# Gated products that stay in PSUM, and 512-token products with the second weights, in a two-layer diffusion block

## The chip, the cores and the metric

The kernel runs on one core of one Trainium2 chip, in one launch. The metric is the device time of that core in microseconds (us); lower is better. Three timed runs of the kernel before the change gave 1726.34, 1726.85 and 1729.16 us, a median of 1726.85. The profile is of one further execution, which took 1731.67 us.

The engines are TensorE (PE in the profile; its weight loads are PEld), VectorE (DVE), ScalarE (ACT), GpSimd (POOL) and SyncE (SP, which issues the transfers). A matmul writes PSUM, 2 KB per partition and bank, eight banks. Everything else lives in SBUF. In this kernel GpSimd is given SBUF operands only.

## The reference, cut to what matters

Two layers over 512 latent tokens and 256 context tokens, 1024 features. Each layer mixes tokens (Fourier, retention and neighbourhood attention) and then runs a gated feed-forward with 2816 inner features:

```python
def swiglu(h, w1, w3, w2):
    return (jax.nn.silu(h @ w1) * (h @ w3)) @ w2

x = x + ga_f * swiglu(rmsnorm(x, g_ffn[i]) * (1.0 + sc_f) + sh_f, w1[i], w3[i], w2[i])
```

The first layer does this for latent and context tokens (768), the last for the 512 latent tokens alone. All inputs and outputs are fp32.

## The kernel before, in words

**Precision.** Every fp32 operand is split into a high part, a cast to the matmul's fp32r type, and a low part, the operand less the high part. `mm3` (L398 to L400) then runs three matmuls: high by high, low by high, high by low. Splitting a weight tile is one ScalarE cast (L183) and one subtraction (L188), on GpSimd for most tiles and on VectorE for a few that a table names.

**The two first weights.** The feed-forward's 22 chunks of 128 inner features go in parts of two or four chunks (`FFN_PARTS`: the second part of the first layer and the fifth of the last have two, all others four). For each part, the weight is taken in two by two blocks (halves of the 1024 features by two chunks) and the tokens in two halves, and each of `w1` and `w3` is multiplied by the seven-product scheme of Strassen and Winograd. A job is one weight's pair of chunks; its products come in the order 1, 2, 6, 7, 4, 5, 3 (`STEPS`). Each product is four `mm3`, twelve matmuls, over n tokens: n is 384 in the first layer and 256 in the last. The weight sums that the scheme needs are formed on VectorE (L225 to L229) before they are split.

**After a product.** `complete` (L1586 on) takes each product out of its PSUM bank. Product 1 is copied to SBUF by ScalarE (L1592). Products 6 and 7 are added to the running sums U (L1596, L1599). Products 2, 4, 5 and 3 each finish one block of the result and call `block`; product 5 is also added to U after that (L1604). For `w1`, `block` adds U (L1630) and takes the SiLU on ScalarE (L1631); this is the gate. For `w3` it adds U into a new SBUF tile `gu` (L1634), multiplies that by the gate into a second `gu` (L1635), and `put` splits the outcome into the two halves of `g`: cast on ScalarE (L1461), subtraction (L1462) on VectorE for products 2 and 3 and on GpSimd for products 4 and 5.

**The second weights.** `plain` multiplies a finished part of `g` by `w2` for one eighth m of the output features: for each stream of tokens in `self.out`, one PSUM bank, `mm3` over the part's chunks, and `add_x` (L1658), which adds the scaled result to x. The streams are 512 and 256 tokens in the first layer and 256 and 256 in the last. Eighths 0 and 1 are taken together, stream by stream; 2 to 7 one at a time. The last part of each layer goes through `finish` and `residual` instead (tile `res`).

**Order.** Each engine runs its instructions in the order in which the program emits them. A planner (`in_order`) fixes the order of products; it lets the first products of the next part's jobs go ahead of the `w2` products of a finished part. `WeightStream` emits, as room in a ring of tiles allows, the transfer of each weight, its cast and its subtraction; so on ScalarE the casts of weights and the casts of `g` stand in one queue, and on VectorE the sums for weights, the adds out of PSUM and the subtractions of `g`. In the first layer VectorE also computes the last layer's modulation (L522) between them.

Of the kernel before, what the change touches and what calls it, by code (L numbers as in the profile page):

```python
# [101 lines left out]
class WeightStream:  # L102
# [19 lines left out]
    def add(self, key, ap, callback=None):  # L122
        self.tasks.append((key, callback, len(self.units)))
        self.units.append(ap)
# [219 lines left out]
def run(*gens):  # L344
    for g in gens:
        for _ in g:
            pass


class Kern:  # L350
# [500 lines left out]
    def strips_ahead(self, layer, heads):  # L851

        if heads[0] == 0:
            self.strip_dram = self.dram.tile([4, P, S_END], F32, tag="strips", bufs=2, name=self.nm("strips"))
            self.strip_parts = ((0, S_CC), (S_CX, S_END))
        parts = [x for x in STRIPS if x[0] != "cc"]
        deltas = []
        for name, lo, hi in parts:
            deltas.append(self.act(cols=hi - lo, name="delta"))
            self.nc.sync.dma_start(deltas[-1], self.a["delta"][:, lo:hi])  # L860
        yield
        for h in heads:
            for (name, lo, hi), delta in zip(parts, deltas):
                st = self.act(cols=hi - lo, name="strip")
                run(self.strip_piece(layer, h, name, delta, st))
                yield
                self.nc.sync.dma_start(self.strip_dram[h, :, lo:hi], st)
# [448 lines left out]
    def residual(self, keys, src, x, layer, part, streams, after, norm, order, n, waiting, hook=None, paces=(1, 2, 2, 2), raws=3):  # L1316
# [11 lines left out]
        def one(w, m, st, last, steps=0):  # L1328
            ps = self.ps("res")
            run(self.products(ps, w, src, st, order, order))  # L1330
            if steps:
                norm.step(steps)
            put(ps, m, st)
            if last:
                self.w.done(keys[m])
# [3 lines left out]
        for ps, w, m, st in waiting:  # L1339
            if hook:  # L1340
                hook()
            run(self.products(ps, w, src, st, order[n:], order))
            put(ps, m, st)
            if st is streams[-1]:
                self.w.done(keys[m])
# [18 lines left out]
class FeedForward:  # L1364
# [134 lines left out]
    def prepare(self):  # L1499
# [10 lines left out]
        for i in range(5):  # L1510
            if i < 4:
                ts = [(j, self.scaled(rs, st, j)) for j in (i, i + 4)]
            if i > 0:
                b11, b12, b21, b22 = (block(e, i - 1) for e in range(4))
                v.tensor_sub(b11, b12, b11)
                t2 = self.k.tmp(name="T2")[:, :n]
                v.tensor_sub(t2, b22, b11)
            if i < 4:
                for j, t in ts:
                    self.shifted(t, st, j)  # L1520
            if i > 0:
                hi, lo = self.operand(6, i - 1)
                nc.scalar.copy(hi, t2)
                nc.gpsimd.tensor_sub(lo, t2, hi.bitcast(F32))  # L1524
                nc.gpsimd.tensor_sub(b21, b21, t2)
            yield 0
        for i in range(4):
            v.tensor_sub(block(1, i), block(3, i), block(1, i))
        del b11, b12, b21, b22, t2, t, ts
        for p, e in ((7, 1), (4, 2), (5, 0), (3, 3)):  # L1530
            for i in range(4):
                self.put(self.operand(p, i), block(e, i), i % 2)
                if p == 5:
                    self.h[i] = None
                elif p == 3:
                    self.h[i + 4] = None
            yield 0
# [46 lines left out]
    def complete(self, job, p, ps):  # L1584

        if p == 6 and job.key in self.waiting:  # L1586
            self.complete(job, 2, self.waiting.pop(job.key))
        add = self.k.nc.vector.tensor_add
        ps, u = ps[:, : self.n], job.u
        if p == 1:  # L1590
            u[2] = self.place(job, 0)
            self.k.nc.scalar.copy(u[2], ps)  # L1592
        elif p == 2:
            self.block(job, 0, 0, ps, u[2])
        elif p == 6:
            add(u[2], u[2], ps)  # L1596
        elif p == 7:
            u[3] = self.place(job, 1)
            add(u[3], u[2], ps)  # L1599
        elif p == 4:  # L1600
            self.block(job, 1, 0, ps, u[3])
        elif p == 5:
            self.block(job, 1, 1, ps, u.pop(3))
            add(u[2], u[2], ps)  # L1604
        else:
            self.block(job, 0, 1, ps, u.pop(2))

# [14 lines left out]
    def block(self, job, r, c, ps, u):  # L1622

        k, n = self.k, self.n
        nc = k.nc
        x, q, i = job.key
        sl = slice(n * c, n * c + n)
        gate = self.gate(job, r)[:, sl]
        if x == "w1":
            nc.vector.tensor_add(gate, ps, u)  # L1630
            nc.scalar.activation(gate, gate, AF.Silu)  # L1631
            return
        t, g = (k.tmp(name="gu")[:, :n] for _ in range(2))
        nc.vector.tensor_add(t, ps, u)  # L1634
        nc.vector.tensor_mul(g, t, gate)  # L1635
        if c == 1:
            del self.gates[q, i, r]
        self.put([self.chunk(q, self.parts[q][1] * r + i, p)[:, sl] for p in range(2)], g, r == 1)

    def chunk(self, q, pos, half):  # L1640

# [20 lines left out]
    def plain(self, q, ms):  # L1662

        k = self.k
        ws = [k.w.get(("w2", self.layer, q, m)) for m in ms]
        size = self.parts[q][1]
        order = sorted(range(2 * size), key=lambda i: i % size)
        for st in self.out:
            sl = slice(st[0], st[0] + st[1])
            for m, w in zip(ms, ws):  # L1670
                ps = k.ps("f2")
                for i in order:
                    c = slice(P * i, P * i + P)
                    k.mm3(
                        ps[:, : st[1]],
                        (w[0][:, c], w[1][:, c]),
                        [self.chunk(q, i, p)[:, sl] for p in range(2)],
                        i == order[0],
                        i == order[-1],
                    )  # L1680
                self.add_x(ps, m, st)
        del ws, w
        for m in ms:
            k.w.done(("w2", self.layer, q, m))

    def run(self, acc, hook=None):


        k = self.k
        self.cur, self.waiting, self.gates = None, {}, {}  # L1690
        k.w.max_raws, k.w.max_parts = 5, 6
        k.w.lead, k.w.dve = DVE[self.layer]
        todo = self.order[:-NK]
        self.first_products()
        for i, (job, p) in enumerate(todo[2 * self.lead :]):
            if i % 2:
                next(self.prep, None)
            if i == SPARE_AT:
                k.w.spare = SPARE if self.last else 0
            if i == 5:  # L1700
                acc.clear()
                if self.layer == 0:
                    k.silu_tables()
            if job.key[0] == "m":

                if p != 1:
                    self.plain(job.key[1], (p,) if p else (0, 1))
            else:
                self.product(job, p)
                if job is todo[-1][0]:  # L1710
                    del self.t[p]
                    if hook and p == 6:
                        hook()
# [449 lines left out]
def _layout(x, c, ctx, c_ctx, w_ada, b_ada, g_mix, w_in, ret_decay_logit, ret_norm_g, w_four,  # L2163
# [45 lines left out]
    wf = w_four.reshape(n, 2, P, 256).transpose(0, 2, 1, 3).reshape(n, P, 512)  # L2209
    o["w_four"] = np.concatenate([wf, np.broadcast_to(dft64, (n, P, 256))], axis=-1)  # L2210
    rows = np.concatenate([np.arange(256), 256 + plain, np.arange(640, 1024)])
    o["w_out"] = A(w_out[:, rows].reshape(n, 8, P, P, NK).transpose(0, 4, 2, 1, 3).reshape(n, NK, P, 1024))
    o["w1"], o["w3"] = chunks(w1), chunks(w3)
# [33 lines left out]
```

## Time and profile before

| What | Value |
|---|---|
| Timed runs, median (lowest to highest) | 1726.85 us (1726.34 to 1729.16) |
| Profiled execution | 1731.67 us |
| Its span | 1729.9 us |
| TensorE matmuls busy | 1620.8 us (94%) |
| VectorE busy | 1219.4 us (70%) |
| GpSimd busy | 876.6 us (51%) |
| ScalarE busy | 743.9 us (43%) |
| Mean granted TensorE clock | 0.976 |

Busy time of TensorE counts a matmul from its start to its modelled end, and successive matmuls overlap, so the number that tells its pace is the distance between starts. The feed-forward of the first layer runs from about 470 to 1010 us of the span, that of the last from about 1340 to the end.

### The profile page before, as it was taken

To read this page: it belongs to the slowest core of one execution; us is meant where nothing else is said; L and a number is where in the kernel's file an instruction comes from. 1 tells how busy PE (TensorE), PEld (TensorE's weight loads), DVE (VectorE), ACT (ScalarE), POOL (GpSimd) and SP (SyncE) were. 2 spreads that over 40 slices of the span, in tenths; PEclk is the share of its full clock that TensorE was granted. 3 is DMA by queue.
4 is the path that set the end of the run, shared out by engine and by line. 5 is a ranking of instruction groups with operands and counts; after the bars stand their busy time and mean duration, and the time that the engine had idled before them with its cause. 6 is when DMAs were issued, how large, how long until landed. Compare 5 with 4: busy or idle time off the path is not lost. (4 is left out here: it accounts for less than half of the span.)

```text
span 1729.9 us, 27017 instructions
## 1 busy us (share of the span) xinstructions
PE 1620.8 (94%) x10054; PEld 1474.1 (85%) x10054; DVE 1219.4 (70%) x2040; ACT 743.9 (43%) x1437; POOL 876.6 (51%) x645
## 2 busy tenths in 40 slices
PE   6989999999979997999999999999998799999997
PEld 4867788879878987898989997788788699999997
DVE  6866566762887899586877867665767876767585
ACT  5544445653643323242333553444545544334343
POOL 3333232123575657465666832543145777667673
PEclk9999999999989999999999999999999899999998
DMA  9354253452123343344343444422141232232222
GB/s 347 137 196 135 69 154 96 117 196 99 37 69 115 95 159 106 116 131 126 134 134 116 148 164 132 143 72 89 62 147 52 71 123 86 74 110 86 79 85 70
DMA packets 76387, 202.33 MB, mean 117 GB/s; under 512 B 12704, under 2 KB 19488, under 8 KB 75872
## 3 DMA queue, kind: packets, MB, share of 16 engines
q1 hardware_dynamic: 76256, 200.60, 35.7%
q8 instruction: 80, 1.31, 0.3%
q14 instruction: 51, 0.42, 0.1%
HBM read 184.25 MB, written 11.80 MB: 113 GB/s over the span
## 5 line engine op out<-in xcount | busy, mean ns | idle before, releaser
L188 POOL TENSOR_TENSOR wp<-wr,wp 128x512 fp32r<-128x512 f32 (+1 forms) x336 | 476.7, 1431 | 277.3 <-ACT wp L183 275.3
L399 PE MATMUL f<-hp,wp 128*128 128x384 f32 (+1 forms) x1232 | 386.7, 314 | 14.5 <-POOL wp L188 8.5
L398 PE MATMUL f<-hp,wp 128*128 128x384 f32 (+1 forms) x1232 | 386.1, 313 | 14.3 <-DVE U L1599 5.3
L400 PE MATMUL f<-hp,wp 128*128 128x384 f32 (+1 forms) x1232 | 384.8, 312 | 4.4 <-POOL hp L1524 4.0
L183 ACT CAST wp<-wr 128x512 fp32r<-128x512 f32 (+1 forms) x360 | 212.9, 607 | 354.9 <-PE f L400 114.7
L188 POOL TENSOR_TENSOR wl<-wr,wh 128x1024 fp32r<-128x1024 f32 (+2 forms) x75 | 163.9, 2190 | 347.7 <-ACT wh L183 278.8
L399 PEld LDWEIGHTS f<-hp,wp 128*128 128x128 f32 x1232 | 237.4, 193 | 20.3 <-POOL wp L188 13.6
L398 PEld LDWEIGHTS f<-hp,wp 128*128 128x128 f32 x1232 | 237.5, 193 | 17.6 <-issue 9.8
L400 PEld LDWEIGHTS f<-hp,wp 128*128 128x128 f32 x1232 | 237.4, 193 | 5.8 <-POOL hp L1524 5.1
L398 PE MATMUL f<-g,wp 128*128 128x256 f32 (+1 forms) x576 | 183.8, 319 | 13.1 <-ACT g L1461 12.8
L400 PE MATMUL f<-g,wp 128*128 128x256 f32 (+1 forms) x576 | 183.6, 319 | 4.8 <-POOL g L1462 4.2
L399 PE MATMUL f<-g,wp 128*128 128x256 f32 (+1 forms) x576 | 182.6, 317 | 0.0
L398 PE MATMUL proj<-h,wh 128*128 128x512 f32 (+1 forms) x456 | 165.0, 362 | 1.0 <-DVE v L404 1.0
L399 PE MATMUL proj<-h,wl 128*128 128x512 f32 (+1 forms) x456 | 159.2, 349 | 0.7 <-POOL wl L188 0.7
L400 PE MATMUL proj<-h,wh 128*128 128x512 f32 (+1 forms) x456 | 158.9, 348 | 0.0
L1658 DVE SCALAR_TENSOR_TENSOR x<-f,mod,x 128x256 f32<-128x256 f32 (+1 forms) x160 | 83.9, 546 | 83.4 <-PE f L400 83.4
L398 PEld LDWEIGHTS f<-g,wp 128*128 128x128 f32 x576 | 113.4, 197 | 22.3 <-ACT g L1461 15.5
L400 PEld LDWEIGHTS f<-g,wp 128*128 128x128 f32 x576 | 113.0, 196 | 13.6 <-POOL g L1462 4.8
L399 PEld LDWEIGHTS f<-g,wp 128*128 128x128 f32 x576 | 113.4, 197 | 6.0
L522 DVE CUSTOM_DVE_ANT_0 adj<-wr,tab 128x1024 bf16<-128x1024 f32 x64 | 105.8, 1671 | 10.0 <-DMA wr<-in_w_adat_dram 10.0
L398 PEld LDWEIGHTS proj<-h,wh 128*128 128x128 f32 x456 | 86.6, 190 | 25.6 <-issue 5.7
L399 PEld LDWEIGHTS proj<-h,wl 128*128 128x128 f32 x456 | 86.8, 190 | 11.8 <-POOL wl L188 1.1
(252 smaller groups left out, 3505.7 us busy)
## 6 DMA issues: line engine op xcount, KB each, us to landing
wr<-in_w_dram SPq DMA_DIRECT2D x88, 512.0 KB
wr<-in_w_adat_dram SPq DMA_DIRECT2D x48, 512.0 KB
wr<-in_w_dram SPq DMA_DIRECT2D x80, 256.0 KB
wr<-in_w_ada_dram SPq DMA_DIRECT2D x32, 512.0 KB
ada<-in_w_ada_dram SPq DMA_DIRECT2D x16, 512.0 KB
wr<-in_w_out_dram SPq DMA_DIRECT2D x16, 512.0 KB
tab<-in_rpb_dram SPq DMA_DIRECT2D x12, 512.0 KB
strip<-strips SPq DMA_DIRECT2D x3, 1152.0 KB
```

Source lines behind the costliest of these rows:

```text
L183: nc.scalar.copy(hi, src)
L188: (nc.vector if vector else nc.gpsimd).tensor_sub(lo, src, hi.bitcast(F32))
L398: mm(out, a[0], b[0], start=start, stop=False)
L399: mm(out, a[1], b[0], start=False, stop=False)
L400: mm(out, a[0], b[1], start=False, stop=stop)
L522: self.nc.vector.tensor_tensor_reduce(out=self.tmp(mybir.dt.bfloat16, D, "adj"), in0=raw, in1=self.tabs[("silu", s)], scale=1.0, scalar=0. ...
L1658: k.nc.vector.scalar_tensor_tensor(xs, ps[:, :n], k.mod[:, self.layer, 5, s, m : m + 1], xs, op0=OP.mult, op1=OP.add)
```

## The change

Three edits, all in the feed-forward.

1. `block` for `w3` no longer uses the two `gu` tiles: the add of U and the product with the gate are written back into the product's own PSUM bank, and `put` casts and subtracts from that bank. The subtraction is on VectorE for all four blocks (the last argument is False).
2. Product 5's add to U comes before its `block`, since the block now overwrites the bank.
3. `plain` takes both streams as one of 512 tokens where they fit (the last layer) for eighths 2 to 7. Eighths 0 and 1 and the first layer stay as they were.

```diff
         elif p == 5:
+            add(u[2], u[2], ps)
             self.block(job, 1, 1, ps, u.pop(3))
-            add(u[2], u[2], ps)
...
-        t, g = (k.tmp(name="gu")[:, :n] for _ in range(2))
-        nc.vector.tensor_add(t, ps, u)
-        nc.vector.tensor_mul(g, t, gate)
+
+        nc.vector.tensor_add(ps, ps, u)
+        nc.vector.tensor_mul(ps, ps, gate)
         if c == 1:
             del self.gates[q, i, r]
-        self.put([self.chunk(q, self.parts[q][1] * r + i, p)[:, sl] for p in range(2)], g, r == 1)
+        self.put([self.chunk(q, self.parts[q][1] * r + i, p)[:, sl] for p in range(2)], ps, False)
...
-        for st in self.out:
+
+        whole = [(0, 2 * self.n)] if 2 * self.n <= 512 and ms[0] > 0 else self.out
+        for st in whole:
```

## Rows read from the trace of the kernel before

**Rows 1.** Windows: stretch, length; busy us of the engines, granted clock, DMA share, GB/s.
```profile
540.00:960.00 420.00, 404.12 (x2273) 378.48 (x2272) 324.17 (x458) 129.74 (x242) 253.72 (x174) 0.99 0.39 124
1340.00:1400.00 60.00, 48.05 (x347) 45.98 (x346) 48.41 (x71) 29.19 (x65) 47.93 (x41) 0.89 0.25 81
1400.00:1690.00 290.00, 279.34 (x2265) 277.47 (x2264) 203.47 (x333) 114.73 (x239) 200.93 (x155) 0.98 0.29 93
```

**Rows 2.** Waits of PE, 1400 to 1700: total us, times, longest.
```profile
PE f L398 <- ACT g L1461: 4.7, 3, 1.8
PE f L400 <- POOL g L1462: 4.2, 3, 1.4
```

**Rows 3.** Waits of PE, 540 to 960.
```profile
PE f L398 <- ACT g L1461: 7.3, 4, 4.1
```

**Rows 4.** Waits of PE, 1340 to 1420.
```profile
PE f L398 <- DVE gate L1630: 3.0, 2, 2.2
```

**Rows 5.** Windows: one change of part in the last layer.
```profile
1520.00:1540.00 20.00, 17.15 (x129) 16.74 (x128) 14.31 (x23) 8.06 (x17) 15.07 (x13) 0.91 0.44 145
```

**Rows 6.** Timeline of PE in the first layer: start us, us, instruction.
```profile
687.20 0.39 PE L398 MATMUL f<-g,wp 128*128 128x512 f32 x1
...
688.35 0.40 PE L400 MATMUL f<-g,wp 128*128 128x512 f32 x1
...
700.01 0.28 PE L400 MATMUL f<-g,wp 128*128 128x256 f32 x1
...
702.53 0.28 PE L400 MATMUL f<-g,wp 128*128 128x256 f32 x1
```

**Rows 7.** Lines by shape, DVE: count | busy us, mean ns | idle before, releasers.
```profile
L1635 DVE TENSOR_TENSOR gu<-gu,gate 128x384 f32<-128x384 f32 x44 | 45.1, 1026 | 4.1 <-ACT gate L1631 1.8
L1634 DVE TENSOR_TENSOR gu<-f,U 128x384 f32<-128x384 f32 x44 | 24.3, 552 | 11.1 <-ACT U L1592 7.1 <-PE f L400 2.6
L1635 DVE TENSOR_TENSOR gu<-gu,gate 128x256 f32<-128x256 f32 x44 | 36.6, 833 | 2.7 <-ACT gate L1631 0.3
L1634 DVE TENSOR_TENSOR gu<-f,U 128x256 f32<-128x256 f32 x44 | 18.5, 421 | 17.8 <-ACT U L1592 12.9 <-PE f L400 2.5 <-DVE U L1604 0.5
L1658 DVE SCALAR_TENSOR_TENSOR x<-f,mod,x 128x256 f32<-128x256 f32 x120 | 55.3, 479 | 51.0 <-PE f L400 51.0
L1658 DVE SCALAR_TENSOR_TENSOR x<-f,mod,x 128x512 f32<-128x512 f32 x40 | 29.8, 747 | 32.4 <-PE f L400 32.4
```

**Rows 8.** Lines by shape, ACT: a copy out of PSUM.
```profile
L1592 ACT COPY U<-f 128x256 f32<-128x256 f32 x20 | 7.3, 367 | 0.0
```

**Rows 9.** Tile gu: count, duration ns least/median/most, first and last start.
```profile
L1635 DVE TENSOR_TENSOR gu<-gu,gate x88: 424/1004/1670, 494.1 to 1698.7; 128x384 f32<-128x384 f32 x44, 128x256 f32<-128x256 f32 x44
L1462 DVE TENSOR_TENSOR g<-gu,g x44: 424/967/1656, 495.8 to 1699.7; 128x384 fp32r<-128x384 f32 x22, 128x256 fp32r<-128x256 f32 x22
L1462 POOL TENSOR_TENSOR g<-gu,g x44: 739/1012/1995, 510.5 to 1699.7; 128x384 fp32r<-128x384 f32 x22, 128x256 fp32r<-128x256 f32 x22
```

**Rows 10.** Timeline of DVE before one change of part in the last layer.
```profile
1503.79 1.43 DVE L1462 TENSOR_TENSOR g<-gu,g 128x256 fp32r<-128x256 f32 x1 [0.71 <-ACT g L1461]
...
1517.43 0.42 DVE L1634 TENSOR_TENSOR gu<-f,U 128x256 f32<-128x256 f32 x1 [2.93 <-ACT U L1592]
```

**Rows 11.** Timeline of POOL at the same change of part.
```profile
1516.38 5.43 POOL L188 TENSOR_TENSOR wp<-wr,wp 128x512 fp32r<-128x512 f32 x4 [0.73 <-ACT wp L183]
...
1525.77 1.83 POOL L1462 TENSOR_TENSOR g<-gu,g 128x256 fp32r<-128x256 f32 x2
```

**Rows 12.** Timeline of ACT there.
```profile
1521.84 0.62 ACT L183 CAST wp<-wr 128x512 fp32r<-128x512 f32 x1 [1.66 <-POOL wp L188]
...
1524.38 0.71 ACT L1461 CAST g<-gu 128x256 fp32r<-128x256 f32 x2
```

**Rows 13.** Timeline of PE there.
```profile
1524.83 0.39 PE L398 MATMUL f<-g,wp 128*128 128x256 f32 x1 [1.44 <-ACT g L1461]
...
1526.74 0.39 PE L400 MATMUL f<-g,wp 128*128 128x256 f32 x1 [1.41 <-POOL g L1462]
```

## Prediction

> **What bounds the kernel now.** I read the stage table first, then the waits of TensorE in the feed-forwards, then the timeline of one stall. In the body of both feed-forwards TensorE is nearly always busy: 404 of 420 us in the first layer, 279 of 290 in the last, while VectorE has 324 and 203 and GpSimd 254 and 201 [rows 1]. So work taken off VectorE or GpSimd is worth nothing by itself there; it counts where TensorE waits for it. The exception is the start of each feed-forward, where TensorE has 48 of 60 us and VectorE as much [rows 1].
>
> The waits that bear on this change are those on `g`. In the last layer TensorE stands three times for the high part (4.7 us) and three times for the low part that GpSimd makes (4.2 us) [rows 2], in the first layer four times for the high part, 7.3 us [rows 3]. They lie where a part of `g` is finished and its `w2` products begin. One of them in full: 20 us hold 129 matmul starts at a granted clock of 0.91 [rows 5]. At the full-rate distance of 0.120 us (2.52 us over 21 steps of 256 tokens [rows 6]) there would be 167; the 38 that are missing cost 4.6 us. [...]
>
> Why TensorE waits there: block 4's cast of `g` runs at 1524.38, because ScalarE stood until 1521.84 for a weight's subtraction on GpSimd, and had one more weight to cast after that [rows 12]; GpSimd was in four weight subtractions of 5.43 us, and began the two of `g` only at 1525.77 [rows 11].
>
> **The change, part by part.**
>
> *Wider matmuls.* The last layer's five parts that go through `plain` have 4, 4, 4, 4 and 2 chunks, 18 together. Six eighths by 18 chunks by 3 is 324 pairs of 256-token matmuls that become 324 of 512. At full clock 512 tokens take 0.230 us (1.15 us over five steps) against 2 times 0.120 [rows 6]: 0.010 us each, 3.2 us in all, on the path, as TensorE is the bound. The lower bound is 0, if a lowered clock or a late `g` covers it; the upper is about 4, as the starts are read to 0.01 us, which over five steps is 0.002 us a matmul. I take 3.2. [...]
>
> *Wider adds to x.* 60 adds of 479 ns become 30 of 747 [rows 7]: 6.3 us less VectorE, hidden behind TensorE either way. Nothing.
>
> *The product with the gate.* It is the one step with both inputs in SBUF: 1026 and 833 ns on average against 552 and 421 for the add beside it, whose one input is PSUM [rows 7], and it ranges from 424 to 1670 ns [rows 9]. At its least it is as short as the PSUM form, so the rest is delay, most likely from GpSimd working in SBUF meanwhile. No row here has VectorE writing PSUM. From below I bound it by 421 ns (the add that reads PSUM), from above by 833 (no gain); I take the add's time, as the nearest row in operation, shape and input. The gain is 0.47 us for each of 44 and 0.41 for each of 44: 39 us of VectorE.
>
> *The subtraction.* VectorE has 44 at about 0.97 us, GpSimd 44 at about 1.01 [rows 9]. After it VectorE has 88 at 0.42 or 0.55, the PSUM form: 43 us, as much as its 44 now. GpSimd loses 44 us. But each subtraction stands behind its cast (about 0.37 us out of PSUM [rows 8], plus the hand-over, 0.45 together), so VectorE waits 44 more times, some 20 us. What is queued behind: the next add out of PSUM, and the weight sums L225 to L229, for which ScalarE's casts wait.
>
> *Product 5.* The add to U comes 0.45 us before its block instead of after it. The sum on VectorE is unchanged; the block is later by that.
>
> *The banks.* A bank of a `w3` block is now free after the add, 0.42 us; then after add, product, cast and subtraction, about 1.75 us in the last layer (three times 0.42, 0.37, and hand-overs). Eight banks at 12 times 0.120 = 1.44 us a product turn over in 11.5 us, so 1.3 us more is covered, except at the start, where product 2's banks are held aside and TensorE already waits for VectorE (3.0 us on L1630 [rows 4]). There the two new subtractions with their waits (2 times 0.87) about cancel the four shorter products (4 times 0.41). I charge 0.5 us for each layer, bounds -1 and +2 each.
>
> *The stall at a change of part, last layer.* The VectorE queue before it: the last subtraction of the pair before ends at 1505.2, having waited 0.71 and taken 1.43 [rows 10]. It becomes about 1.3 us shorter, the three products before it 1.2, and two new subtractions cost 1.7: the queue is 0.8 us ahead. The next product with the gate gives 0.4. ScalarE's copy of U, for which VectorE stood 2.93 us [rows 10], sits behind the same weights, so all of this moves up by about 1.2 us: block 4's cast to 1523.1. Its subtraction follows on VectorE at once, and the low part is there at 1523.9 instead of 1526.7. TensorE, which arrives at 1523.4, waits about 0.5 instead of 2.85 us. What is late next is block 3: behind block 4's subtraction VectorE does block 5 (two adds, product, cast, subtraction, 2.1 us) and block 3 (1.75 us), ready at 1527.7, high part at 1527.3. TensorE wants it after 21 more matmuls, at 1526.4: a new wait of about 1 us. Waits fall by 1.3 us, and of the 1.7 us lost to the clock I expect half back: 2.2 us a stall, 6.6 for three. Bounds 0 and 4.6 each.
>
> The last part (`residual`) gains as much early and loses as much on block 3: 0, between -1 and +1.
>
> *The stalls in the first layer.* There a `w2` stream of 512 tokens spans both 384-token halves, so block 3 is wanted at once. Its product and its subtraction get shorter by 0.5 and 0.4; blocks 5 and 4 put two more subtractions in front of it, partly in time in which VectorE waits for a transfer anyway. Between 3.6 gained and 8.4 lost (twice 0.55 and 0.51 for each of four); I take 2.0 gained, as nearer to the rows of the shorter product.
>
> *Sum.* 3.2 + 6.6 + 2.0 - 1.0 = 10.8 us off 1731.67, 1720.9 for an execution like the profiled one. That lies 4.8 above the median of the timed runs, 1726.85; the same step from the median gives 1716.
>
> **The rivals.**
>
> *Only the matmuls pay.* The stall moves from block 4 to block 3 at the same length, or the in-place operations take as long as now. For it: VectorE does blocks 4, 5 and 3 strictly in turn, with a cast inside each. Against it: the product's least time, 424 ns. It gives 3.2 less: 1723.6. [...]
>
> *Slower.* VectorE's own queue becomes the bound at a change of part. If block 4's cast comes no sooner than 1524.38, block 3 is ready at 1529 where TensorE wants it at about 1527: 2.3 us in place of 1.41, 0.9 more at each of four stalls, 3.6. In the first layer two more subtractions with casts, 2.1 us, at each of five changes: 10.5. With 1 for the starts and 3.2 off: 11.9 more, 1739. It decides if ScalarE's casts of `g` are not moved up. For it: VectorE is at 77% in the first layer [rows 1]. Against it: GpSimd loses 44 us of the very queue that holds ScalarE.
>
> *Much faster.* The waits on `g` go altogether and the clock stays up: 3 times 4.6, 7.3 in the first layer with 1.5 more of clock, and 3.2: 26 less, 1701. [...] Against it: block 3.
>
> **How the numbers follow.** A measurement of this kernel can tell about 0.2%, 3.5 us, from no change. My forecast has 0.50, with a range of its own from 1708 to 1722; only the matmuls 0.22 (1721 to 1727), slower 0.12, much faster 0.16. The range 1703 to 1730 leaves out most of the slower case and the far end of the faster one. Faster takes the forecast, the much faster case and half of the second: 0.77. Same takes the other half of the second and a small share of the slower: 0.12. Slower 0.11.
>
> **What would show it.** Right: L1635 at about 0.42 and 0.55 us with a narrow spread; no subtraction of `g` on POOL, and its busy time about 44 us lower; 324 starts of 512 tokens at 0.230 us; the waits on POOL for `g` gone; a wait for L1461 or L1462 on block 3 after some thirty `w2` matmuls. Wrong: L1635 still near 1 us; starts of 512 tokens at other distances; longer waits on L1630 or L1599 at the starts, or TensorE waiting for weights because L225 comes later.

## Result and the profile after

The changed kernel takes 1701.55 us (median of 4 runs, 1700.14 to 1703.79) where the kernel before takes 1727.5 beside it (4 runs): 26 us less, ratio 0.9844 [0.9826, 0.9862]. Measured again, beside more runs of the kernel before (e13 below): 1704.25 against 1731.31, 0.9847 [0.9832, 0.9863]. The forecast was 1716 with a range from 1703 to 1730. The time lies just below that range, on the rival that I had given 0.16: "much faster", 1701.

The profiled execution took 1700.14 us, its span 1698.4. PE is busy for 1601.1 us (before 1620.8), with 9730 matmuls where it had 10054, 324 fewer as counted; VectorE 1178.8 (1219.4), GpSimd 818.6 (876.6). The stage table again, in the columns of [rows 1] (after the length come the busy times of TensorE, its weight loads, VectorE, ScalarE and GpSimd, each with its count, then the clock, the DMA share and GB/s); the second row is moved by 14 us, so that it begins as far behind the last layer's first `w2` product as the row of before does, and the third is the change of part of [rows 5], moved to its new place:

```profile
540.00:960.00 420.00, 410.14 (x2319) 387.32 (x2318) 316.66 (x482) 134.69 (x253) 238.22 (x165) 0.99 0.40 129
1386.00:1676.00 290.00, 283.60 (x2061) 269.63 (x2060) 196.75 (x343) 122.02 (x258) 192.31 (x146) 0.99 0.29 90
1499.15:1519.15 20.00, 19.36 (x117) 17.10 (x116) 12.43 (x20) 8.12 (x17) 12.77 (x10) 1.00 0.29 93
```

TensorE is busy 6 us more in the first layer's stretch and 4 in the last's. At the change of part the granted clock was 0.91 on average, since it stood at 0.50 from 1528.0 to 1531.4 us; now it is 1.00 throughout.

TensorE's waits, first from 530 to 960 us, to be set against [rows 3]:

```profile
PE f L399 <- POOL wp L188: 4.3, 6, 0.9
PE f L398 <- ACT g L1461: 3.5, 2, 1.8
PE f L398 <- ACT wp L183: 2.0, 2, 1.0
```

Before, the same window held

```profile
PE f L398 <- ACT g L1461: 8.1, 5, 4.1
PE f L399 <- POOL wp L188: 6.1, 8, 1.1
```

The changed kernel's waits from 1388 to 1700 us, to be set against [rows 2]:

```profile
PE res L398 <- DVE g L1462: 2.7, 2, 1.6
PE f L398 <- ACT g L1461: 1.8, 3, 0.6
PE res L398 <- ACT g L1461: 1.5, 1, 1.5
```

In the last layer 8.9 us in six waits have become 1.8 in three, and the waits for GpSimd's low part are gone. On the lines named `res`, in the last part, TensorE now waits 4.2 us in three: for the subtractions of blocks 2 and 4 and for block 3's cast. Before it waited 2.3 us there in two:

```profile
PE res L398 <- DVE U L1596: 1.7, 1, 1.7
PE res L400 <- POOL g L1462: 0.6, 1, 0.6
```

VectorE's operations by shape, against [rows 7] and [rows 9]:

```profile
L1658 DVE SCALAR_TENSOR_TENSOR x<-f,mod,x 128x512 f32<-128x512 f32 x70 | 51.5, 745 | 45.1 <-PE f L400 45.1
L1635 DVE TENSOR_TENSOR f<-f,gate 128x384 f32<-128x384 f32 x44 | 24.9, 566 | 2.2
L1462 DVE TENSOR_TENSOR g<-f,g 128x384 fp32r<-128x384 f32 x44 | 24.5, 558 | 29.4 <-ACT g L1461 29.4
L1635 DVE TENSOR_TENSOR f<-f,gate 128x256 f32<-128x256 f32 x44 | 19.0, 432 | 1.7
L1462 DVE TENSOR_TENSOR g<-f,g 128x256 fp32r<-128x256 f32 x44 | 18.7, 424 | 33.2 <-ACT g L1461 33.2
```

Writing a PSUM bank in place costs little more than the add out of PSUM did (552 and 421 ns, [rows 7]): 566 and 432 ns for the product that took 1026 and 833.

The three stalls that the prediction was mostly about, at the same change of part as [rows 10] to [rows 13]: VectorE, ScalarE, TensorE.

```profile
1494.18 0.43 DVE L1634 TENSOR_TENSOR f<-f,U 128x256 f32<-128x256 f32 x1 [2.31 <-ACT U L1592]
...
1497.37 0.43 DVE L1635 TENSOR_TENSOR f<-f,gate 128x256 f32<-128x256 f32 x1
1502.01 0.42 DVE L1462 TENSOR_TENSOR g<-f,g 128x256 fp32r<-128x256 f32 x1 [4.21 <-ACT g L1461]
```

```profile
1499.05 0.62 ACT L183 CAST wp<-wr 128x512 fp32r<-128x512 f32 x1 [1.40 <-POOL wp L188]
1501.08 0.62 ACT L183 CAST wp<-wr 128x512 fp32r<-128x512 f32 x1 [1.41 <-POOL wp L188]
1501.60 0.37 ACT L1461 CAST g<-f 128x256 fp32r<-128x256 f32 x1
```

```profile
1501.30 0.28 PE L398 MATMUL f<-g,wp 128*128 128x256 f32 x1
...
1505.70 0.39 PE L398 MATMUL f<-g,wp 128*128 128x256 f32 x1 [0.64 <-ACT g L1461]
...
1508.17 0.40 PE L398 MATMUL f<-g,wp 128*128 128x512 f32 x1
1508.41 0.40 PE L399 MATMUL f<-g,wp 128*128 128x512 f32 x1
```

The part's first `w2` product starts at 1501.30. Block 4's product on VectorE is done at 1497.80, but its cast begins at 1501.60: ScalarE has weight casts ahead of it in its queue, one about every 2.0 us, each behind a weight subtraction on GpSimd. VectorE stands 4.21 us for that cast. Before, the same cast came 2.23 us behind the first `w2` product (1524.38 and 1522.15); now it comes 0.30 behind.

*Where the time came from.* The start times of the matmuls, laid against each other in the two traces, give the length of each stretch of `w2` products. The sums below are over the five stretches of each layer (the last part's beginning, in `residual`, is not in them):

| kernel | first layer, us | last layer, us |
|---|---|---|
| before | 165.5 | 119.4 |
| changed | 154.0 | 101.6 |
| changed, again (e13) | 156.9 | 101.6 |

Between the stretches the products take the same time in both in the last layer (40.5 us between two changes of part) and behind the third stretch of the first (58.4). Behind the first stretch of the first layer they take 1.5 us more: TensorE's wait at the second change of part grew from 0.25 to 1.70 us, and it lies ahead of that part's first `w2` product, so no stretch holds it. Some 3 us of the 31 between the two profiled executions are not the change: they arise before the first feed-forward, and the changed kernel itself differs by 6 us between two executions there. In the first layer the stretches repeat only to about 3 us (its third took 35.55 and 38.50 in the two executions). Whole feed-forwards repeat better; from the last mixer product to the last `res` product, by the matmul starts:

| kernel | first layer, us | last layer, us |
|---|---|---|
| before | 556.0 | 398.7 |
| changed | 546.6 | 380.5 |
| changed, again (e13) | 546.4 | 379.1 |

So the first layer gives 9.5 us and the last 18 to 20. The `res` products themselves took 1.5 us longer in both layers of the first of the two executions (37.3 and 30.7 us against 35.8 and 29.2 before) and as long as before in e13. TensorE's waits in the last layer's are the same in both executions (4.2 us, before 2.3); the granted clock was 0.95 and 0.94 in the first and 1.00 in e13 (before 1.00 and 0.94). So what parts the two executions is the clock, and beside the kernel before the last layer's 1.5 us come with the longer waits. The products just ahead of them in the last layer gained 1.6 us in both.

### The profile page after: what moved, and what is told of

Read it like the earlier page. It is cut to its first block, busy times and chain, and to the rows that moved or that the text cites. A ratio compares the mean times of both kernels' runs of the same rounds, so it can differ in the third digit from the quotient of the medians.

```text
span 1698.4 us, 26272 instructions
## 1 busy us (share of the span) xinstructions
PE 1601.1 (94%) x9730; PEld 1449.0 (85%) x9730; DVE 1178.8 (69%) x2054; ACT 741.9 (44%) x1437; POOL 818.6 (48%) x601
## 5 line engine op out<-in xcount | busy, mean ns | idle before, releaser
L188 POOL TENSOR_TENSOR wp<-wr,wp 128x512 fp32r<-128x512 f32 (+1 forms) x336 | 465.7, 1399 | 311.0 <-ACT wp L183 306.2
L398 PE MATMUL f<-g,wp 128*128 128x512 f32 (+1 forms) x468 | 160.5, 343 | 5.4 <-ACT g L1461 5.4
L400 PE MATMUL f<-g,wp 128*128 128x512 f32 (+1 forms) x468 | 160.5, 343 | 0.0
L399 PE MATMUL f<-g,wp 128*128 128x512 f32 (+1 forms) x468 | 160.3, 342 | 0.0
L1658 DVE SCALAR_TENSOR_TENSOR x<-f,mod,x 128x512 f32<-128x512 f32 (+1 forms) x130 | 79.0, 622 | 69.5 <-PE f L400 69.3
L398 PEld LDWEIGHTS f<-g,wp 128*128 128x128 f32 x468 | 89.1, 190 | 17.0 <-ACT g L1461 6.8
L400 PEld LDWEIGHTS f<-g,wp 128*128 128x128 f32 x468 | 88.9, 190 | 11.2 <-DVE g L1462 1.1
L399 PEld LDWEIGHTS f<-g,wp 128*128 128x128 f32 x468 | 89.1, 190 | 9.9
```

The costliest lines, as they stand in the source:

```text
L188: (nc.vector if vector else nc.gpsimd).tensor_sub(lo, src, hi.bitcast(F32))
L398: mm(out, a[0], b[0], start=start, stop=False)
L399: mm(out, a[1], b[0], start=False, stop=False)
L400: mm(out, a[0], b[1], start=False, stop=stop)
L1658: k.nc.vector.scalar_tensor_tensor(xs, ps[:, :n], k.mod[:, self.layer, 5, s, m : m + 1], xs, op0=OP.mult, op1=OP.add)
```

## Experiments

All are timed in five rounds beside the kernel before. In the diffs "-" is the kernel named in the heading.

### e1: the wider matmuls alone, in the kernel before

```
-        for st in self.out:
+        whole = [(0, 2 * self.n)] if 2 * self.n <= 512 and ms[0] > 0 else self.out
+        for st in whole:
```

> The kernel before with the third edit alone: one stream of 512 tokens for eighths 2 to 7 in the last layer. Theory A (the gain is in the waits for g and in the clock that falls after them; the wide matmuls bring their own 324 times 0.010 us): about 1724, 3 us less, the three waits on ACT L1461 and POOL L1462 in the last layer as long as before (about 9 us together). Rival W (the wide matmuls bring most of it, also by loading fewer weights): 1712 or less.

1726.0 against 1729.17 us, 0.998 [0.9969, 0.9992]: some 3 us less (3.2 by the medians, 3.5 by the ratio). The stalls stay: 5.2 us for the high part and 4.2 for GpSimd's low part in the last layer. The matmuls' own gain is neither lost nor covered, and rival W falls.

### e2: the changed kernel with narrow matmuls

```
-        whole = [(0, 2 * self.n)] if 2 * self.n <= 512 and ms[0] > 0 else self.out
-        for st in whole:
+        for st in self.out:
```

> The kernel after without the third edit: the gated products stay in PSUM, the second weights' products keep their streams of 256 tokens. Theory A: about 1705, 3 us more than the whole change; waits for g as short as with the whole change (under 2 us in the last layer) and a granted clock near 1.00 where a part ends. Rival W: 1714 or more.

1704.7, 0.9864 [0.985, 0.9877]. The in-place products and subtractions bring some 24 us, and the two halves of the change add up.

### e3: only the subtractions moved to VectorE, reading SBUF, in the kernel before

```
-        self.put([self.chunk(q, self.parts[q][1] * r + i, p)[:, sl] for p in range(2)], g, r == 1)
+        self.put([self.chunk(q, self.parts[q][1] * r + i, p)[:, sl] for p in range(2)], g, False)
```

> The kernel before with one thing changed: VectorE subtracts the low part of g for all four blocks; the two SBUF tiles for the sum and the product stay. Theory A (both halves count: GpSimd must lose the subtractions, and VectorE's steps must not run against GpSimd in SBUF): about half of the gain, 1713 to 1718; the product with the gate still near 1 us and the subtraction near 0.9 us on average. Rival S (taking g off GpSimd is all): 1704 to 1708. Rival P (only the short steps matter): 1727 or more, since VectorE then has 44 more contended subtractions, some 40 us.

1745.54, 1.0104 [1.0089, 1.012]: 16 to 18 us slower. Theory A and rival S, which both had a gain, fall; rival P's "1727 or more" holds. The products stay long (893 and 766 ns), the 88 subtractions take 781 and 629. The last layer's stretches sum to 119.3 us, as before; the first layer's to 172.8, 7.3 more. The whole feed-forwards take 13.6 us more in the first layer and 3.3 in the last. TensorE's wait in the first layer, from 530 to 960 us, beside 8.1 in five before:

```profile
PE f L398 <- ACT g L1461: 15.3, 5, 4.8
```

This is the mechanism of my "slower" rival: in the first layer two more subtractions stand on VectorE in front of block 3, and all five waits are for block 3's cast.

### e4: only the product out of PSUM, GpSimd's half of the subtractions kept

```
-        t, g = (k.tmp(name="gu")[:, :n] for _ in range(2))
-        nc.vector.tensor_add(t, ps, u)
-        nc.vector.tensor_mul(g, t, gate)
+        g = k.tmp(name="gu")[:, :n]
+        nc.vector.tensor_add(ps, ps, u)
+        nc.vector.tensor_mul(g, ps, gate)
```

(in the kernel before; product 5's add comes first here too)

> The kernel before with the sum written back to PSUM, the product read from there and written to one SBUF tile, product 5's add moved ahead; the subtraction stays half on GpSimd. So no VectorE step of the block but the subtraction has two SBUF inputs. Theory A: the product with the gate falls to 0.42 and 0.55 us, and about half of the gain comes, 1713 to 1718; the low part of block 4 still comes late from GpSimd. Rival S: 1725 to 1728. Rival P: 1704 to 1708.

1709.56, 0.989 [0.9877, 0.9904]: 19 us of the 26 by this alone, between theory A's 1713 to 1718 and rival P's 1704 to 1708. The 4.9 us from here to e2 are what VectorE's taking over all the subtractions, out of PSUM, brings. The product takes 558 and 424 ns; the stretches sum to 155.7 and 109.3, and the first layer's whole feed-forward takes 546.9 us, as in the changed kernel. In the last layer the high part is no longer waited for; what is left is GpSimd's low part, as before [rows 2]:

```profile
PE f L400 <- POOL g L1462: 4.2, 3, 1.4
```

### e5: the product out of PSUM into SBUF, all subtractions on VectorE out of SBUF

```
-        nc.vector.tensor_mul(ps, ps, gate)
+        g = k.tmp(name="gu")[:, :n]
+        nc.vector.tensor_mul(g, ps, gate)
...
-        self.put([self.chunk(q, self.parts[q][1] * r + i, p)[:, sl] for p in range(2)], ps, False)
+        self.put([self.chunk(q, self.parts[q][1] * r + i, p)[:, sl] for p in range(2)], g, False)
```

(against the changed kernel; narrow matmuls)

> The product reads PSUM and writes SBUF, all four subtractions are on VectorE and read SBUF, narrow matmuls; it stands between the run with the product alone (1709.6) and the changed kernel with narrow matmuls (1704.7). Theory A (VectorE's chain of add, product and subtraction over blocks 5, 4 and 3 at a change of part sets the stalls, and a subtraction that reads SBUF is drawn out by GpSimd to about 0.75 us): 1708 to 1713, the stalls of the first layer longer than in the changed kernel. Rival G (what counts after the product is that GpSimd has no subtraction of g any more, whatever VectorE reads): 1702 to 1706.

1718.83 against 1729.12, 0.9933 [0.9917, 0.9949]. Rival G falls: to free GpSimd of `g` is not worth anything by itself. Theory A has the direction but not the size: it is 7 us slower than e4, not level with it. Against e2 the one difference is where `g` lies when it is cast and subtracted, SBUF or PSUM, and that is 0.7%, 12 us. The subtraction takes 762 and 564 ns here, 558 and 424 there. (The profiled execution is the fastest of the six, 1713.54 us, so its waits and stretches flatter this kernel.)

```profile
L1462 DVE TENSOR_TENSOR g<-gu,g 128x384 fp32r<-128x384 f32 x44 | 33.5, 762 | 29.9 <-ACT g L1461 29.9
L1462 DVE TENSOR_TENSOR g<-gu,g 128x256 fp32r<-128x256 f32 x44 | 24.8, 564 | 34.1 <-ACT g L1461 34.1
```

### e9: the changed kernel with every product formed twice

```
+        nc.vector.tensor_mul(k.tmp(name="gx")[:, :n], ps, gate)
         nc.vector.tensor_mul(ps, ps, gate)
```

> The changed kernel with one more VectorE operation ahead of each of the 88 products, the same product written to a spare tile in SBUF: some 43 us more VectorE, each 0.42 or 0.55 us long and as little drawn out as the product itself. Theory A (the length of VectorE's chain is what counts): it gives back most of what the shorter product brought, 1713 to 1722. Rival G (the gain is that GpSimd and VectorE no longer draw each other out in SBUF, and VectorE's own time is hidden): 1701 to 1706.

1721.79, 0.9952 [0.9935, 0.9968]: some 19 us back, at the upper end of theory A's span; rival G falls for the kernel as a whole. But the two layers differ. The first layer's stretches sum to 166.4 (154.0 to 156.9 without), and all of the gain there is gone; the last layer's to 103.1, 1.5 more. From 530 to 970 us:

```profile
PE f L398 <- ACT g L1461: 12.0, 5, 3.5
```

The whole feed-forwards tell the same: VectorE has 24.6 us more work in the first layer and that layer takes 17 us longer; in the last it has 18.7 more, and that layer takes 4 to 5 longer. So VectorE's own time sets the first layer, and in the last layer three quarters of it are hidden.

### e7: 512 tokens in eighths 0 and 1 too

```
-        whole = [(0, 2 * self.n)] if 2 * self.n <= 512 and ms[0] > 0 else self.out
+        whole = [(0, 2 * self.n)] if 2 * self.n <= 512 else self.out
```

> The changed kernel, with 512 tokens for eighths 0 and 1 too. Theory A (block 3 is what is late next, since it comes about 4.4 us after the first second-weight product of a part and is now wanted after 1.4 us): the wait grows from 0.6 to about 3.6 us at each of three changes of part, +8 us and more if the clock falls there, 1708 to 1714. Rival H (VectorE is ahead by then and block 3 not late): 54 more wide pairs at 0.010 us, 1700 to 1701.5.

1710.97, 0.989 [0.9873, 0.9907]: 8 us slower than the changed kernel. From 1388 to 1700 us:

```profile
PE f L398 <- ACT g L1461: 8.4, 3, 2.8
```

The three waits grow from 0.6 to 2.8 us, as theory A had it (3.6). Block 3 is what is late next, and the two narrow eighths are what covers it.

### e8: blocks 4 and 5 of each layer's last part as before the change

```
-        nc.vector.tensor_add(ps, ps, u)
-        nc.vector.tensor_mul(ps, ps, gate)
+        old = q == len(self.parts) - 1 and r == 1
+        t, g = (k.tmp(name="gu")[:, :n] for _ in range(2)) if old else (ps, ps)
+        nc.vector.tensor_add(t, ps, u)
+        nc.vector.tensor_mul(g, t, gate)
...
-        self.put([self.chunk(q, self.parts[q][1] * r + i, p)[:, sl] for p in range(2)], ps, False)
+        self.put([self.chunk(q, self.parts[q][1] * r + i, p)[:, sl] for p in range(2)], g, old)
```

> The changed kernel, but blocks 4 and 5 of each layer's last part go through SBUF tiles and GpSimd's subtraction as before. Theory A (in the last part the banks that wait for the cast and subtraction are what costs 1.3 us in each layer): 1698.5 to 1700.5. Rival F (the loss there is GpSimd's or ScalarE's lateness on block 3, which this makes worse): 1702 to 1705.

1705.44, 0.9859 [0.9843, 0.9875]; its interval overlaps the changed kernel's. Theory A's 1698.5 to 1700.5 did not come, and rival F's 1702 to 1705 is just passed. In the last layer's last part TensorE waits 2.0 us for GpSimd and 1.5 for VectorE, instead of 2.7 for VectorE and 1.5 for ScalarE. Inconclusive on the cause; there is nothing to be had this way.

### e11: the whole change in the last layer alone

```
-        nc.vector.tensor_add(ps, ps, u)
-        nc.vector.tensor_mul(ps, ps, gate)
+        t, g = (ps, ps) if self.last else (k.tmp(name="gu")[:, :n] for _ in range(2))
+        nc.vector.tensor_add(t, ps, u)
+        nc.vector.tensor_mul(g, t, gate)
...
-        self.put([self.chunk(q, self.parts[q][1] * r + i, p)[:, sl] for p in range(2)], ps, False)
+        self.put([self.chunk(q, self.parts[q][1] * r + i, p)[:, sl] for p in range(2)], g, r == 1 and not self.last)
```

(and product 5's add behind its block in the first layer)

> The whole change in the last layer alone, the first layer as before. From the lengths of the second-weight phases in the traces, the last layer alone should give 15 to 18 us of the 27, so 1709 to 1713 beside 1729. Rival: the first layer gives most, and this is over 1716.

1714.38 against 1731.31, 0.9909 [0.9896, 0.9923]: 16 to 17 us, in the gain that was expected. The other 10 us of the 27 on this chip are the first layer's.

### e13: the changed kernel again, beside e10 to e12

> The changed kernel again, beside the others on one chip: 1701 to 1704.

1704.25, 0.9847 [0.9832, 0.9863], just above what was expected.

### e10: VectorE makes the high part of `g` itself, last layer

```
-        self.put([self.chunk(q, self.parts[q][1] * r + i, p)[:, sl] for p in range(2)], ps, False)
+        hi, lo = [self.chunk(q, self.parts[q][1] * r + i, p)[:, sl] for p in range(2)]
+        (nc.vector.tensor_copy if self.last else nc.scalar.copy)(hi, ps)
+        nc.vector.tensor_sub(lo, ps, hi.bitcast(F32))
```

> The changed kernel, but in the last layer VectorE itself makes the high part of g from the PSUM bank, where ScalarE's cast stood (one more operation of about 0.42 us in place of a wait of 0.44). Theory Q (in the last layer the stalls come from ScalarE's queue, where a cast of g stands behind weight casts that GpSimd paces): VectorE no longer waits 4.2 us ahead of block 4's subtraction, the 0.6 us waits on block 3 go, and the last part ends up to 1.5 us sooner; 1.5 to 4 us less than the changed kernel. Rival A (VectorE's own chain sets them): no gain or up to 3 us slower.

1693.31 against 1731.31, 0.9782 [0.9766, 0.9798]: 11 us less than the changed kernel on the same chip, and the fastest kernel here. Rival A falls. Theory Q stands, but I had the gain too small. The stretches of the last layer sum to 98.4 (101.6), with no wait left inside them; most of the rest comes from the last part's `res` products, 4.0 us shorter than in e13 and 5.5 shorter than in the first profile, where I had put 1.5. VectorE's 44 copies and 44 subtractions, all in PSUM's form, cost 18.7 us each, and it hardly waits any more (33.2 us for the casts in the changed kernel):

```profile
L1639 DVE CAST g<-f 128x256 fp32r<-128x256 f32 x44 | 18.7, 424 | 1.5
L1640 DVE TENSOR_TENSOR g<-f,g 128x256 fp32r<-128x256 f32 x44 | 18.7, 424 | 1.6
```

### e12: the same in both layers

```
-        (nc.vector.tensor_copy if self.last else nc.scalar.copy)(hi, ps)
+        nc.vector.tensor_copy(hi, ps)
```

(against e10)

> As the run with VectorE's cast in the last layer, in both layers. Theory A for the first layer (VectorE is the bound there, at a change of part): its copies of 0.55 us take the place of waits of 0.44 us and of waits on weight casts, so the first layer is the same within 2 us; the whole 1.5 to 4 us less than the changed kernel. Rival: the copies add up on VectorE, and the first layer loses 4 to 8 us.

1695.14, 0.9789 [0.9773, 0.9806]: level with e10. In the first layer the copies of VectorE and the waits for ScalarE weigh about the same (156.5 us of stretches, the whole feed-forward 3 us less, where theory A had the same within 2); the whole gains more than it gave for the reason told under e10.

### e14: e10's edit in the kernel before, where everything lies in SBUF

```
-        self.put([self.chunk(q, self.parts[q][1] * r + i, p)[:, sl] for p in range(2)], g, r == 1)
+        hi, lo = [self.chunk(q, self.parts[q][1] * r + i, p)[:, sl] for p in range(2)]
+        (nc.vector.tensor_copy if self.last else nc.scalar.copy)(hi, g)
+        (nc.gpsimd if r == 1 else nc.vector).tensor_sub(lo, g, hi.bitcast(F32))
```

> The kernel before, with one edit: in the last layer VectorE makes the high part of g, in place of ScalarE's cast; product, tiles and GpSimd's half of the subtractions stay. Theory Q alone (ScalarE's queue with weight casts in it is the whole of the last layer's stalls): most of what the change won there, 12 to 17 us less than before, with block 4's high part at about 1.2 us after a part's first second-weight product in place of 2.23. Theory QV (ScalarE's queue and the drawn-out products on VectorE each hold part of it): 3 to 9 us less, the low part of block 4 or block 3 still awaited. Theory V (VectorE's products alone): within 3 us of before, or slower by the added copies.

1751.79 against 1730.47, 1.0113 [1.0096, 1.013]: about 20 us slower. What took 11 us off in PSUM costs 20 in SBUF (where GpSimd also keeps its half of the subtractions and the matmuls are narrow). Theory Q alone falls, and QV too; V's "slower by the added copies" is what came, far beyond its 3 us. The last layer's stretches sum to 132.7 (119.4). VectorE at a change of part, then GpSimd beside it:

```profile
1535.19 1.40 DVE L1639 CAST g<-gu 128x256 fp32r<-128x256 f32 x1
...
1537.72 0.30 DVE L1639 CAST g<-gu 128x256 fp32r<-128x256 f32 x1
...
1538.91 1.44 DVE L1635 TENSOR_TENSOR gu<-gu,gate 128x256 f32<-128x256 f32 x1
1540.38 1.25 DVE L1639 CAST g<-gu 128x256 fp32r<-128x256 f32 x1
1541.66 1.37 DVE L1640 TENSOR_TENSOR g<-gu,g 128x256 fp32r<-128x256 f32 x1
```

```profile
1535.19 1.26 POOL L188 TENSOR_TENSOR wp<-wr,wp 128x512 fp32r<-128x512 f32 x1 [0.81 <-ACT wp L183]
1536.68 0.73 POOL L1640 TENSOR_TENSOR g<-gu,g 128x256 fp32r<-128x256 f32 x1 [0.23 <-DVE g L1639]
1538.10 0.73 POOL L1640 TENSOR_TENSOR g<-gu,g 128x256 fp32r<-128x256 f32 x1 [0.69 <-DVE g L1639]
1538.78 3.97 POOL L188 TENSOR_TENSOR wp<-wr,wp 128x512 fp32r<-128x512 f32 x3
```

Each VectorE operation here has all its operands in SBUF, and each that starts beside a GpSimd operation ends 0.15 to 0.3 us after that one does: 1536.59 after 1536.45, and the last three, one behind another, after the three of 1.32 us. The one copy between two GpSimd operations takes 0.30 us.

## Why the prediction was wrong

*What held.* The product at 0.43 and 0.57 us with no spread, VectorE taking over the subtraction in the PSUM form (88 at 0.42 or 0.56), 324 pairs of matmuls less at 0.23 us, the wider adds for nothing, and the wide matmuls' 3.2 us (3.2 to 3.5 in e1, about the same from e2 to the changed kernel). Block 3 is what is late next (0.6 us where I had 1; e7). The last part was put at 0, between -1 and +1; in the last layer it gained 0.1 and 1.6 us in the two executions, in the first it lost 1.5 and nothing. The starts, charged 0.5 each, lost nothing: between the last mixer product and the first change of part the changed kernel is 0.5 to 0.9 us ahead in each layer.

*The step that failed in the last layer* is "the stall at a change of part": 2.2 us each, 6.6 in all. The last layer's first stretch has no stall; up to the next product it takes 23.04 us before and 22.11 after. Against it the next three, which hold the stalls, lost 6.1, 4.9 and 4.9 us before and lose 1.1 each now. So each stall gave 4.2 on average, close to the upper bound of 4.6, and the three gave 12.5. At the stall of [rows 13] I had a wait of 0.5 left on block 4, and there is none; of 1.0 on block 3, and it is 0.64; and half of the clock's 1.7. Behind the waits two things were off.

First, I took the mean saving of the product, 0.4 us, for "the next product with the gate", and 1.2 for the three before it. The mean is over two kinds. Of the 44 products of 256 columns before, the 16 that started with GpSimd idle took 424 to 426 ns; the 28 that started beside a GpSimd operation averaged 1065, and 27 of them ended 278 to 285 ns after that operation did, however long it still had to run. After, both kinds take 432. At this very change of part they took, before,

```profile
1517.89 1.32 DVE L1635 TENSOR_TENSOR gu<-gu,gate 128x256 f32<-128x256 f32 x1
...
1522.14 0.43 DVE L1635 TENSOR_TENSOR gu<-gu,gate 128x256 f32<-128x256 f32 x1
...
1522.93 1.16 DVE L1635 TENSOR_TENSOR gu<-gu,gate 128x256 f32<-128x256 f32 x1
...
1524.99 1.11 DVE L1635 TENSOR_TENSOR gu<-gu,gate 128x256 f32<-128x256 f32 x1
```

Block 4's product now starts 3.93 us ahead of the first `w2` product; before it started 0.01 ahead of it. I had moved it by 1.2. (The product was also not the one step with both inputs in SBUF: the subtraction L1462 is another, from 424 to 1656 ns in [rows 9].)

Second, I let the cast follow VectorE: "all of this moves up by about 1.2 us". But the last thing ahead of that cast is a weight cast on ScalarE, in both kernels. Afterwards that is the one at 1501.08 shown above; before, it was

```profile
1523.85 0.62 ACT L183 CAST wp<-wr 128x512 fp32r<-128x512 f32 x1 [1.39 <-POOL wp L188]
```

The cast moved by 1.93 us, and VectorE's product then lies done for 3.8 us. e9 shows the same from the other side: 0.43 us more VectorE in each block cost the last layer's stretches 1.5 us in all; and e10 takes ScalarE out of the chain and wins 11 us. VectorE alone can hold the part too, if its operations are long enough: e14 has no cast of `g` on ScalarE there, and loses 20 us.

What moved the weight casts is not settled. Counted from the first `w2` product, the seven weight casts ahead of block 4's came 1.6 to 2.8 us earlier. The first of the seven stands on ScalarE behind a SiLU that waits for VectorE's add (L1630), and that add came 1.6 us earlier too, 10.9 us ahead instead of 9.3:

```profile
1512.89 0.76 DVE L1630 TENSOR_TENSOR gate<-f,U 128x256 f32<-128x256 f32 x2
...
1490.45 0.42 DVE L1630 TENSOR_TENSOR gate<-f,U 128x256 f32<-128x256 f32 x1
```

(before and after). So VectorE's shorter queue would be most of the 1.93, where I had it 0.8 ahead; e4, which leaves GpSimd and ScalarE their work and ends the waits for the high part, fits that. Against it: in e9 the add is only 9.5 us ahead, and block 4's cast still comes 0.05 us behind the first `w2` product. No run changed the queue alone.

Of the clock I expected "half back", half of 1.7 us a stall. No run shows that term as a time of its own; it was my estimate, what the two waits of [rows 13] leave of the 4.6 us of a stall. What the trace of before shows is a granted clock of 0.50 for 3.4 us at two of the three stalls and for 6.8 us at the first. All of it came back: from 1355 to 1668 us of the changed kernel the clock is 1.00, also behind the three waits of up to 0.6 us that are left.

*The step that failed in the first layer* is the account of block 3, 2.0 us gained. The whole feed-forward gave 9.5, e11 by difference 10. I counted the shorter product of block 3 and two more subtractions with their casts in front of it, 2.1 us, but not that blocks 5 and 4, in the same VectorE queue, have shorter products as well, an estimated 0.5 each by the means of [rows 7]. Counted from the part's first `w2` product, block 3's cast came 1.3 to 3.5 us earlier at four of the five changes of part. e4, with the product alone, brings the first layer to 546.9 us, where the whole change has 546.5, so nearly all of it is the product. With the subtraction in SBUF the two added ones do cost what I feared (e3, 7.3 us more in the stretches; e5, 160.2 us of them where e4 has 155.7); in PSUM they cost nothing.

*The rivals.* "Much faster" was right in size, and its price (26) was worked out from the same rows. In part that is luck: it let all the waits on `g` of the first layer go, for 8.8 us with their clock; 3.5 of 8.1 us of waits stayed, and the layer gave 9.5 all the same. I gave it 0.16 because block 3 spoke against it, and in the last layer block 3's wait was only 0.6. "Slower" named a real mechanism (e3, e14), with the wrong condition: not that ScalarE's casts fail to move up, but that the operations stay in SBUF. Its sum took four stalls in the last layer, where [rows 2] have three; with three it is 1738.

I had only supposed that GpSimd delays the product, without splitting its records. Split, they show it: at 256 columns and with both inputs in SBUF, 1065 ns on average beside a GpSimd operation and 424 to 426 without one, and with one input in PSUM 432 in both cases. e14's copies between SBUF tiles show the same, 1.22 us against 0.29 to 0.30.

## What to carry to other kernels

Before an operation is priced at its mean, split its records by what the neighbour engine did when it started: a mean of 833 ns hid 425 and 1065, and long ones lay on the path. Where VectorE works beside a busy GpSimd, keep one operand in PSUM (the product took 432 ns there, GpSimd busy or not), and only then move more work to VectorE: the same copy on VectorE was 11 us faster there and 20 slower in SBUF. After a stall goes, ask which queue holds the same tile next; here it was ScalarE's, and a copy on VectorE that costs about as much as the wait for ScalarE's cast (0.42 and 0.44 us) took off another 0.7%.

## What the runs showed of the hardware

An SBUF to SBUF copy of 128x256 on VectorE took 0.29 to 0.30 us in the 13 cases where GpSimd was idle at its start, and 1.22 us on average (up to 1.40) in the 31 where it was not (e14); out of PSUM it took 0.42 in all 44, in 40 of them beside a GpSimd operation (e10). A product written back into the PSUM bank that it reads takes 8 ns more than one written to SBUF (432 and 424 at 256 columns, e4). And the granted clock stayed at 1.00 through a change of part with one wait of 0.64 us, where before two waits of 1.4 us with a few matmuls between them were followed by 3.4 us at 0.50 (0.91 on average over 20 us). In e4, with a single wait of 1.4 us at each change of part, it was 0.99 over 1400 to 1690 us (0.98 before). The waits of the last part, 1.1, 1.6 and 1.5 us, were followed by 3.4 us at 0.50 in one execution of the changed kernel (0.94 on average over the last layer's `res` products) and by none in the other (1.00).
